# Hawk and HGRN2 trunk step: gate products as row tiles, Silu gates, two projections added in DRAM, the first layer's order searched as a whole

## The chip, the cores and the metric

The kernel runs on one core of one Trainium2 chip. The metric is the device time of one execution in microseconds (us). Engines: PE is the matrix engine (PEld its weight loads), DVE the vector engine, ACT the activation engine, POOL the general engine, SP the queue that issues most transfers.

## What is computed

One inference step of two layers over 1024 tokens of a new sequence and 8 sequences of 4 tokens each, 1056 columns in all, in float32. The first layer ("layer 1" in the title; `l0` in the code) is a recurrent one of width 1536 with gates that are block-diagonal, 16 blocks of 96; the second (`l1`) is a gated linear recurrence with matrix states. The change lies in the first.

```python
u = xn @ w_in                                   # 1024 -> 2 * 1536
xb, gate = u[..., :W_LRU], u[..., W_LRU:]
xc, new_buf = _causal_conv(xb, conv_w, conv_b, buf)
# _rg_lru, with xh = xc as 16 blocks of 96
r  = sigmoid(einsum('btni,nij->btnj', xh, w_r) + b_r)
ig = sigmoid(einsum('btni,nij->btnj', xh, w_i) + b_i)
log_a = -LRU_C * softplus(-lam) * r
a = exp(log_a)
bterm = sqrt(-expm1(2.0 * log_a)) * (ig * xc)
h = scan of h_t = a_t * h_(t-1) + bterm_t
y = h * silu(gate)
x = x + y @ w_out                               # 1536 -> 1024
```

## The kernel before

Everything is held with channels on the 128 partitions and tokens along the rows: `x` is 8 tiles of 128 x 1056, cut into three chunks `c` of 352 columns (`CH`). Each float32 operand is split into a high and a low part, and a product is three matmuls, high by high, high by low, low by high (`mm3`, lines 269 to 271). A block of 1024 x 128 weights is loaded in two transfers, its high part is made by a copy on ACT (L418) and its low part by a subtraction on POOL or DVE (L358).

The 1536 channels of the first layer are worked through in four groups `g` of 384, that is three tiles `j` of 128. For each group: `conv(g)` and `gate(g)` project the normalized input (24 matmuls to an output tile and chunk, psum banks `mm`, four of them); `lru(g)` does the gates and the recurrence; `split_y(g)` splits the result; `out(g)` multiplies by the group's rows of `w_out`, for groups 0 and 1, and `out_last` does groups 2 and 3 together.

The gates in `lru`. A group is four blocks of 96. Tile `j` holds block `j` in 96 of its rows and a third of the fourth block in the other 32 (rows 32j to 32j+31). For each chunk and each of the two gates (`i`), three products of 128 x 128 weights (`gh`, `gl`, with zeros where rows of the fourth block stand) use the three tiles of `X`; a fourth of 96 x 96 (`gsh`, `gsl`) uses the rows of the fourth block, which transfers have first gathered in `G4` (L344, six per chunk). Each product has its own bank of the four `hg`, and ACT takes it out with a Tanh (L618, L624). Then ACT does Exp, Tanh and a Sqrt (L631, L633, L641), DVE and POOL the products around them, and DVE the scan (L658).

The output gate (`gate`, L574 and 575) is ACT's Tanh of half the value and DVE's (t + 1) times the value; the missing factor 0.5 comes in where the state is multiplied on (L668). Where the input's norm is not known yet (`by`) or the state is there already (`late`), there are two DVE instructions.

`out(g, src, dst)` (L682 ff.): for each of 8 output tiles and 3 chunks, a product of 9 matmuls into an `mm` bank, a load of the running sum's chunk from DRAM, DVE's add from psum (L689), and a store. Group 0 reads the input and writes `x1a`, group 1 reads `x1a` and writes `x1b`, `out_last` reads `x1b`.

The order of everything is not that of the code. Each step is recorded in a `Flow` with its engine, an estimated duration, what it reads and writes and a priority. `plan` plays the steps through with these durations, one queue for each engine, and so makes an order; `run` repeats that eight times with keys from a pass backwards, then `search` shifts keys in the first 60 us at random, 3000 times, and keeps what gets more of PE's work done by then. The instructions are written out in that order on each engine. `plan` takes Tanh, Exp and Silu for one table of ACT and Sqrt for another, with 1.29 us for a swap (`SETS`, `SWAP`); a product of the gates is 0.48 us of PE.

Of the kernel before, what the change touches and what calls it, by code (L numbers as in the profile page):

```python
# [25 lines left out]
SEARCH = 3000  # L26
NW, NXO, NRAW = 4, 3, 3
# [27 lines left out]
class Flow:  # L55
# [56 lines left out]
    def plan(self, key, horizon=None):  # L112
# [13 lines left out]
        for _ in range(n):  # L126
# [84 lines left out]
    def run(self, tries=0, first=0.0):  # L211
        self.after = [[] for _ in self.ops]
        for i, o in enumerate(self.ops):
            for d in o[3]:
                self.after[d].append(i)
        best = got = self.plan([o[4] for o in self.ops])
        for _ in range(self.TURNS):
            got = self.plan(self.back(got[2], got[4]))
            self.ends.append(got[0])
            best = min(best, got, key=lambda g: g[0])  # L220
        if tries:
            best = self.search(best, tries, first)
        self.log = [(i, self.ops[i][0], best[1][i], best[2][i]) for i in best[3]]
        for i in best[3]:
            self.ops[i][2]()
# [12 lines left out]
def tile_trunk(ctx: ExitStack, tc: tile.TileContext, xT, prm, hc, w0, wg, wo0, w1, wo1, s_in,  # L238
# [91 lines left out]
    with ExitStack() as l0:  # L330
# [59 lines left out]
        G4 = fixed("G4", [96, NCH, CH], F32R)  # L390
# [164 lines left out]
        def gate(g, js=range(3), late=False):  # L555

            items = []
            for j in js:

                def evac(c, ps, pk, by=None, j=j):  # L560
                    sg, sk = sgs[g][j, c] = halves[g % 2][3 * j + c]
                    if late:
                        t, tk = next(ts)
                        act(CH, lambda: S.activation(t, ps[:, :CH], AF.Tanh, scale=0.5), (pk,), (tk,), 0)
                        dve(CH, lambda: V.scalar_tensor_tensor(t, t, 1.0, ps[:, :CH], op0=ALU.add, op1=ALU.mult), (pk, tk), (tk,), 0)
                        dve(CH, lambda: V.scalar_tensor_tensor(sg, sg, 0.5, t, op0=ALU.mult, op1=ALU.mult), (tk, sk), (sk,), 1, True)
                        return
                    if by:
                        t, tk = next(ts)
                        dve(CH, lambda: V.tensor_tensor(sg, ps[:, :CH], by[0], op=ALU.mult), (pk, by[1]), (sk,), 0)  # L570
                        act(CH, lambda: S.activation(t, sg, AF.Tanh, scale=0.5), (sk,), (tk,), 0)
                        dve(CH, lambda: V.scalar_tensor_tensor(sg, t, 1.0, sg, op0=ALU.add, op1=ALU.mult), (tk, sk), (sk,), 1, True)
                        return
                    act(CH, lambda: S.activation(sg, ps[:, :CH], AF.Tanh, scale=0.5), (pk,), (sk,), 0)  # L574
                    dve(CH, lambda: V.scalar_tensor_tensor(sg, sg, 1.0, ps[:, :CH], op0=ALU.add, op1=ALU.mult), (pk, sk), (sk,), 0)

                items.append((w0[ML + 3 * g + j], evac))
            return items

        def lru(g):  # L580
# [16 lines left out]
            for c in range(NCH):  # L597
# [6 lines left out]
                for j in range(3):  # L604
# [5 lines left out]
                for i, hb in ((0, hbr), (1, hbi)):  # L610
                    for j in range(3):
                        m = 3 * g + j
                        ps, pk = next(hg)
                        (a, ak), (b, bk) = xpart(j, 0, c), xpart(j, 1, c)
                        u = 3 * i + j
                        fl.add("PE", 0.48, lambda ps=ps, a=a, b=b, u=u: mm3(ps[:, :CH], (gh[:, u, :], gl[:, u, :]), a, b, True, True),
                               (ak, bk, ("gh", u // 4 * 4), ("gl", u // 4 * 4)), (pk,), 0)
                        act(CH, lambda ps=ps, R=R, i=i, j=j, hb=hb, m=m: S.activation(R[:, i, j], ps[:, :CH], AF.Tanh, bias=hb[:, m:m + 1],  # L618
                                                                           scale=0.5), (pk, ("smb",)), (("R", s, i, j),), 2, 0.1)
                    ps, pk = next(hg)  # L620

                    fl.add("PE", 0.48, lambda ps=ps, i=i, both=both: mm3(ps[:96, :CH], (gsh[:, i], gsl[:, i]), *both, True, True),
                           (("gsh",), ("gsl",), *(("g4", j, q) for j in range(3) for q in own)), (pk,), 0)
# [21 lines left out]
                for j in range(3):  # L645
# [22 lines left out]
                    dve(CH, lambda h=h, sg=sg: V.scalar_tensor_tensor(sg, h, 0.5, sg, op0=ALU.mult, op1=ALU.mult), (hk, sk), (sk,), 3, True)  # L668
# [11 lines left out]
        def out(g, src, dst):  # L680

            own = cycle([next(xos) for _ in range(NXO)] + [next(ts) for _ in range(3)] + [(x[:, :CH], k) for x, k in (next(xbs) for _ in range(3))])  # L682
            for m in range(KD):
                w = weights(wo0[m][:, 384 * g:384 * g + 384], 384)
                for c in range(NCH):
                    ps, pk = product(w, ycols(c))
                    x, xk = next(own)
                    dma(x, src[m][:, chunk(c)], ((g, m, c),), (xk,), 3)
                    dve(CH, lambda x=x, ps=ps: V.tensor_tensor(x, ps[:, :CH], x, op=ALU.add), (pk, xk), (xk,), 0)  # L689
                    dma(dst[m][:, chunk(c)], x, (xk,), ((g + 1, m, c),), 3)  # L690
                    yield

# [10 lines left out]
        def out_last(src):  # L703
# [42 lines left out]
            for c in range(NCH):  # L746
                acc = next(xbs)
                rows = []
                for i, m in enumerate(ms[c]):
                    ps, pk = product(blocks[m].get, ycols(c) + xcols(c)[:3], 1)  # L750
                    x, xk = spare[c][m]
                    dma(x, src[m][:, chunk(c)], ((2, m, c),), (xk,), 3)
# [220 lines left out]
        x1b = [nc.dram_tensor(f"x1b_{m}", (128, TOK), F32, kind="Internal").ap() for m in range(KD)]  # L973
# [4 lines left out]
        gates, rest = project0(gate(2)), out(0, xT, x1a)  # L978
# [8 lines left out]
        rest = out(1, x1a, x1b)  # L987
# [8 lines left out]
        out_last(x1b)  # L996
# [4 lines left out]
        with tc.manual_schedule(engines={E.PE, E.DVE, E.Activation, E.Pool, E.SP}):  # L1001
            fl.run(SEARCH, 60.0)


    with ExitStack() as l1:
# [865 lines left out]
        with tc.manual_schedule(engines={E.PE, E.DVE, E.Activation, E.Pool, E.SP}):  # L1871
            fl.run(SEARCH, 60.0)
# [71 lines left out]
```

## Time and profile before

| | |
|---|---|
| three timed runs | 1031.18, 1028.95, 1027.11 us (median 1028.95) |
| profiled execution, first to last instruction | 1027.8 us |
| PE busy in it | 1015.8 us (99%) |
| DVE, ACT, POOL busy | 808.0, 573.2, 504.2 us |
| first layer | to about 518 us |

No separate time is given for the profiled execution; its span is 1.15 us below the median of the timed ones. How to read the rows that follow: a row of a timeline is start, duration, engine, line, operation, what is written from what is read, the weights' rows * columns, the operand's shape and how many such rows were merged into one. In a table of groups, what stands between the bars is busy us and the mean ns of one, and behind the second bar the idle time of the engine just before and what ended it. Waits are: us in total, times, longest. Matmuls overlap, so the pace of PE is the distance between starts and not a duration. A matmul whose operands are plain float32 shows as two records.

### The profile page before, as it was taken

How to read it: one execution, taken by the hardware profiler on the slowest of the kernel's cores; microseconds unless marked ns; L12 is line 12 of the kernel's file. 1: busy time of each engine (PE TensorE's matmuls, PEld its weight loads, DVE VectorE, ACT ScalarE, POOL GpSimd, SP SyncE). 2: the span in 40 equal slices, each digit the busy share in tenths (PEclk: the TensorE clock that was granted, in tenths of full speed). 3: DMA queues.
4: the chain of work that ended last, by engine and by line, in shares of the span. 5: the costliest groups of instructions: out<-in, count | busy, mean ns of one | idle time of the engine just before them, and what ended most of it. 6: DMA issues, size and time to landing. Idle time of an engine off the chain costs nothing.

```text
span 1027.8 us, 26439 instructions
## 1 busy us (share of the span) xinstructions
PE 1015.8 (99%) x10100; PEld 995.2 (97%) x10100; DVE 808.0 (79%) x1640; ACT 573.2 (56%) x1313; POOL 504.2 (49%) x580
## 2 busy tenths in 40 slices
PE   9999999999999999999999999999999999999997
PEld 9999999999999999999999999999999999999986
DVE  7998987689788689344598989888989898986436
ACT  7688566877765766344454463626363545552324
POOL 1324454454446345635425555555565656633544
PEclk9999999999999999999999999999999999999999
DMA  9211112213762487553564245443535353777204
GB/s 303 73 51 37 54 57 66 79 53 104 222 198 70 131 267 241 157 173 130 159 192 136 72 131 149 130 148 112 167 107 172 94 166 114 217 230 229 88 1 169
DMA packets 109582, 139.95 MB, mean 136 GB/s; under 512 B 24208, under 2 KB 86800, under 8 KB 109456
## 3 DMA queue, kind: packets, MB, share of 16 engines
q1 hardware_dynamic: 107440, 135.84, 42.7%
q10 hardware_dynamic: 2016, 2.43, 0.7%
q8 instruction: 79, 1.29, 0.5%
q14 instruction: 47, 0.39, 0.1%
HBM read 90.02 MB, written 41.61 MB: 128 GB/s over the span
## 4 chain that ended last, share of the span: by engine, by line
PE 87%; DVE 4%; DMA 4%; ACT 2%; issue 1%; POOL 1%; SPq 1%; POOLq 0%; ACTq 0%; DVEq 0%
PE mm L269 25%; PE mm L271 24%; PE mm L270 24%; PE hg L1138 2%; DMA R<-td 1%; PE hg L269 1%; PE hg L270 1%; PE hg L271 1%; PE hg L1340 1%; PE hg L1285 1%; PE hg L1342 1%; DMA wraw<-in_w_dram 1%; DMA k<-x1a 1%; SPq L344 1%; DMA R<-in_xT_dram 1%
## 5 line engine op out<-in xcount | busy, mean ns | idle before, releaser
L269 PE MATMUL mm<-xh,whi 128*128 128x352 f32 (+1 forms) x1127 | 349.9, 311 | 0.0
L271 PE MATMUL mm<-xh,wlo 128*128 128x352 f32 (+1 forms) x1127 | 347.8, 309 | 0.0
L270 PE MATMUL mm<-xl,whi 128*128 128x352 f32 (+1 forms) x1127 | 347.7, 309 | 0.0
L358 POOL TENSOR_TENSOR wlo<-wraw,whi 128x256 fp32r<-128x256 f32 (+3 forms) x188 | 201.9, 1090 | 194.6 <-ACT whi L418 93.7
L269 PEld LDWEIGHTS mm<-xh,whi 128*128 128x128 f32 x1127 | 211.7, 188 | 1.2 <-DVE k L1598 0.2
L270 PEld LDWEIGHTS mm<-xl,whi 128*128 128x128 f32 x1127 | 212.3, 188 | 0.4
L271 PEld LDWEIGHTS mm<-xh,wlo 128*128 128x128 f32 x1127 | 212.0, 188 | 0.0
L269 PE MATMUL mm<-t,whi 128*128 128x264 f32 (+1 forms) x330 | 96.6, 293 | 0.0
L544 DVE SCALAR_TENSOR_TENSOR k<-xb,prm_sb,k 128x352 f32<-128x352 f32 (+2 forms) x144 | 87.3, 633 | 10.4 <-ACT k L541 9.6
L271 PE MATMUL mm<-t,wlo 128*128 128x264 f32 (+1 forms) x330 | 94.5, 286 | 0.0
L270 PE MATMUL mm<-t,whi 128*128 128x264 f32 (+1 forms) x330 | 94.3, 286 | 0.0
L1598 DVE TENSOR_TENSOR k<-mm,k 128x264 f32<-128x264 f32 x154 | 64.1, 424 | 11.9 <-PE mm L271 10.5
L358 POOL TENSOR_TENSOR wlo<-R,whi 128x256 fp32r<-128x256 f32 x70 | 57.1, 838 | 27.8 <-ACT whi L1522 24.6
L1522 ACT CAST whi<-wraw 128x512 fp32r<-128x512 f32 x56 | 34.6, 617 | 58.6 <-DVE wraw L1532 31.0
L637 POOL TENSOR_TENSOR k<-X 128x352 f32<-128x352 f32 x36 | 43.8, 1222 | 45.4 <-DVE R L638 33.6
L269 PEld LDWEIGHTS mm<-t,whi 128*128 128x128 f32 x330 | 62.0, 188 | 2.1 <-ACT kt L1355 0.9
L271 PEld LDWEIGHTS mm<-t,wlo 128*128 128x128 f32 x330 | 62.2, 188 | 0.0
L270 PEld LDWEIGHTS mm<-t,whi 128*128 128x128 f32 x330 | 62.1, 188 | 0.0
L418 ACT CAST whi<-wraw 128x512 fp32r<-128x512 f32 (+2 forms) x79 | 43.8, 571 | 27.3 <-PE mm L270 20.0
L269 PE MATMUL mm<-yh,whi 128*128 128x352 f32 x153 | 49.9, 326 | 1.0 <-DVE k L689 1.0
L270 PE MATMUL mm<-yl,whi 128*128 128x352 f32 x153 | 49.4, 323 | 0.0
L271 PE MATMUL mm<-yh,wlo 128*128 128x352 f32 x153 | 49.4, 323 | 0.0
(484 smaller groups left out, 2503.1 us busy)
## 6 DMA issues: line engine op xcount, KB each, us to landing
wraw<-in_w_dram SPq DMA_DIRECT2D x89, 256.0 KB, 3.1
wraw<-in_wo_dram SPq DMA_DIRECT2D x34, 192.0 KB, 2.6
R<-in_w_dram SPq DMA_DIRECT2D x17, 256.0 KB, 3.5
si<-in_s_in_dram SPq DMA_DIRECT2D x8, 512.0 KB, 5.5
vt<-sg SPq DMA_DIRECT2D x8, 512.0 KB, 3.7
kt<-kt SPq DMA_DIRECT2D x8, 512.0 KB, 3.3
sg<-vt SPq DMA_DIRECT2D x32, 128.0 KB, 2.9
kt<-kt SPq DMA_DIRECT2D x32, 128.0 KB, 4.5
```

Of the source, the lines that this page charges most:

```text
L269: T.matmul(out, wh, xh, start=first, stop=False)
L270: T.matmul(out, wh, xl, start=False, stop=False)
L271: T.matmul(out, wl, xh, start=False, stop=last)
L344: fl.add("SP" if q is Q else "ACT", us, lambda: q.dma_start(dst, src), r, w, prio, kb * (1.0 if r else 0.75))
L358: emit = lambda: e.tensor_tensor(b, x, a.bitcast(F32), op=ALU.subtract)
L418: act(m, lambda hi=hi, raw=raw, m=m: S.copy(hi[:, :m], raw[:, :m]), rk, (hk,), prio)
L544: dve(u, lambda src=src, dst=dst, sh=sh, k=k: V.scalar_tensor_tensor(dst, sh(src, k), pc("cw", 12 * k + m), dst, op0=ALU.mult, op1=ALU.add ...
L637: pool(CH, lambda x=x, a=a, b=b: G.tensor_tensor(x, a.bitcast(F32), b.bitcast(F32), op=ALU.add), (ak, bk), (xk,), 3)
L1138: T.matmul(ps[32 * j:32 * j + 32, n * w:n * w + w], B[:, o:o + 32], q(slice(o, o + 32)), start=True, stop=True, tile_position=(0, 32 * j))
L1285: T.matmul(ps[w, n * 128:(n + 1) * 128], kt[:, 4 * i + n, a], vt[:, 4 * i + n], start=True, stop=True, tile_position=(0, 32 * a))
L1522: act(512, lambda: S.copy(hi, raw), (rk,), (hk,), 2)
L1598: dve(QT, lambda: V.tensor_tensor(o[0], z[0], u[0], op=ALU.add), (z[1], u[1]), (o[1],), 0)
```

## The change

Five things, all in the first layer:

- **Gates.** The rows of the array are cut into tiles, so that matmuls on few rows can share a pass. The block-diagonal weights have no zeros multiplied any more: the four products of a chunk and gate become three slots. A slot is one step of PE for the planner (0.48 us) and has three passes (high by high, high by low, low by high). In slots 1 and 2 a pass is two matmuls of 64 rows, in slot 3 four of 32 rows, each with its own bank; the four products are ready when slot 3 is done, and they need all four `hg` banks at once. `G4` needs only two of the three row pieces (four transfers for six); the third is read where it is.
- **Silu.** ACT computes the output gate in one instruction; the factor 0.5 and DVE's part go.
- **Projections.** `out(g)` no longer loads and adds: ACT copies the product out of psum, a transfer stores it in `part[g][m]`, and when three chunks are there, a transfer that adds in DRAM, issued by POOL, adds the tile to `x1a[m]`. `x1a` starts as a copy of the input, by eight transfers from DRAM to DRAM. `x1b` is gone.
- **Search.** `refine` shifts keys of steps of the whole first layer, 3000 times, and keeps an order whose planned end is not later. The second layer has none.
- In the planner, POOL's transfers are no longer held up by DVE's use of the shared memory port.

```diff
+REFINE = 3000, 0
...
-            elif e == "POOL":
+            elif e == "POOL" and not kb:
...
+    def refine(self, best, tries):
+
+        rng, key, end = Random(2), list(best[1]), best[0]
+        free = [i for i, o in enumerate(self.ops) if o[4] >= 0]
+        for _ in range(tries):
+            t, w = rng.uniform(0.0, best[0]), rng.choice((5.0, 10.0, 20.0))
+            near = [i for i in free if abs(key[i] - t) < w]
+            if not near:
+                continue
+            new = list(key)
+            for i in rng.sample(near, min(len(near), rng.randint(1, 6))):
+                new[i] += rng.gauss(0.0, rng.choice((2.0, 6.0, 15.0)))
+            got = self.plan(new)
+            if got[0] <= end + 1e-9:
+                end, key = got[0], list(got[1]) if rng.random() < 0.5 else new
+                best = min(best, got, key=lambda g: g[0])
+        return best
...
-                    act(CH, lambda: S.activation(sg, ps[:, :CH], AF.Tanh, scale=0.5), (pk,), (sk,), 0)
-                    dve(CH, lambda: V.scalar_tensor_tensor(sg, sg, 1.0, ps[:, :CH], op0=ALU.add, op1=ALU.mult), (pk, sk), (sk,), 0)
+                    act(CH, lambda: S.activation(sg, ps[:, :CH], AF.Silu), (pk,), (sk,), 0)
...
-                for j in range(3):
+                for j in range(2):
...
                 for i, hb in ((0, hbr), (1, hbi)):
+                    got = [next(hg) for _ in range(4)]
+                    xs = [[xpart(j, p, c) for p in range(2)] for j in range(3)]
+                    four = [(both[p], [("g4", j, own[p]) for j in range(2)]) for p in range(2)]
+
+                    def slot(*tiles, i=i, got=got, first=False, last=False):
+
+                        cells, r = [], []
+                        for b, x, rows in tiles:
+                            q = slice(*rows)
+                            w = (gsh[q, i], gsl[q, i]) if b == 3 else (gh[q, 3 * i + b, :], gl[q, 3 * i + b, :])
+                            cells.append((got[b][0][:96 if b == 3 else 128, :CH], *w, x[0][0][q], x[1][0][q], rows[0]))
...
+                        def emit():
+                            for k, (u, v) in enumerate(((1, 3), (1, 4), (2, 3))):
+                                for t in cells:
+                                    T.matmul(t[0], t[u], t[v], start=first and not k, stop=last and k == 2, tile_position=(t[5], 0))
+
+                        fl.add("PE", 0.48, emit, r, [got[b][1] for b, _, _ in tiles], 0)
+
+                    slot((2, xs[2], (0, 64)), (0, xs[0], (64, 128)), first=True)
+                    slot((1, xs[1], (64, 128)), (3, four, (0, 64)), first=True)
+                    slot((1, xs[1], (0, 32)), (0, xs[0], (32, 64)), (3, xs[2], (64, 96)), (2, xs[2], (96, 128)), last=True)
...
-                    dma(x, src[m][:, chunk(c)], ((g, m, c),), (xk,), 3)
-                    dve(CH, lambda x=x, ps=ps: V.tensor_tensor(x, ps[:, :CH], x, op=ALU.add), (pk, xk), (xk,), 0)
-                    dma(dst[m][:, chunk(c)], x, (xk,), ((g + 1, m, c),), 3)
+                    act(CH, lambda x=x, ps=ps: S.copy(x, ps[:, :CH]), (pk,), (xk,), 0)
+                    dma(part[g][m][:, chunk(c)], x, (xk,), (("part", g, m, c),), 3)
                     yield
+                fl.add("POOL", 1.0, lambda m=m: G.dma_start(x1a[m], part[g][m], accum_op=ALU.add, max_dma_last_dim=8192),
+                       [("part", g, m, c) for c in range(NCH)], [("x1a", m)], 5, 540)
...
+        for m in range(KD):
+            dma(x1a[m], xT[m], (("xh", m, 2),), (("x1a", m),), 6, 700)
```

PE before, at the gates of the first group: products of the gates (`hg`, from `X`) stand between those of a convolution tile (`mm_159`).

```order
L271 MATMUL mm_159<-xh_97,X_142 128x352
L269 MATMUL hg_163<-X_142,gh_117 128x352 [waits Activation_49]
L270 MATMUL hg_163<-X_142,gh_117 128x352
L271 MATMUL hg_163<-X_142,gl_118 128x352
L269 MATMUL hg_164<-X_142,gh_117 128x352 [waits Activation_49]
L270 MATMUL hg_164<-X_142,gh_117 128x352
L271 MATMUL hg_164<-X_142,gl_118 128x352 [waits Pool_49]
```

All of them use the whole array. PE in the change, the last slot of 64 rows in a run and the start of the slot of 32 rows (L646 is the matmul of a slot; `hg_161` to `hg_164` are the four banks, `gh` and `gl` the weights' parts):

```order
L646 MATMUL hg_161<-X_142,gl_118 128x352
L646 MATMUL hg_163<-X_142,gl_118 128x352
L646 MATMUL hg_164<-X_142,gh_117 128x352
L646 MATMUL hg_163<-X_142,gh_117 128x352
L646 MATMUL hg_162<-X_142,gsh_119 96x352
L646 MATMUL hg_161<-X_142,gh_117 128x352
L646 MATMUL hg_164<-X_142,gh_117 128x352
```

Two matmuls to a pass have become four. A run of L646 is mostly a whole set of 24 (15 times); the 576 of them stand in 34 runs, between matmuls on all rows.

ACT before, in the gates of the first group (L574 is the Tanh of the output gate, L631 Exp, L633 Tanh, L618 and L624 take the gates out of psum):

```order
L574 ACTIVATE sg_147<-mm_159 128x352
L631 ACTIVATE a_114<-R_73,smalls_84 128x352 [waits DMAHW1_49]
L618 ACTIVATE R_73<-hg_164,smalls_84 128x352 [waits PE_49]
L618 ACTIVATE R_73<-hg_161,smalls_84 128x352 [waits PE_49]
L624 ACTIVATE td_116<-hg_162,smalls_84 96x352 [waits PE_49]
L633 ACTIVATE R_73<-R_73,smalls_84 128x352 [waits Activation_49]
L574 ACTIVATE sg_145<-mm_160 128x352
```

No table load stands between them. ACT in the change, at a like place later in the layer (L592 is Silu, L656 and L659 take the gates out of psum, L666 is Exp, L668 Tanh, L676 Sqrt):

```order
L666 ACT_TABLE_LOAD [waits DMAHW5_49]
L666 ACTIVATE a_114<-R_73,smalls_84 128x352 [waits Activation_49]
L666 ACTIVATE a_114<-R_73,smalls_84 128x352 [waits DMAHW6_49,Activation_49]
L656 ACTIVATE R_73<-hg_161,smalls_84 128x352 [waits DMAHW4_49,PE_49]
L666 ACTIVATE a_114<-R_73,smalls_84 128x352 [waits DMAHW0_49,Activation_49]
L659 ACTIVATE td_116<-hg_162,smalls_84 96x352
L668 ACTIVATE R_73<-R_73,smalls_84 128x352 [waits Activation_49]
L656 ACTIVATE R_73<-hg_164,smalls_84 128x352
L668 ACTIVATE R_73<-R_73,smalls_84 128x352
L656 ACTIVATE R_73<-hg_163,smalls_84 128x352
L592 ACT_TABLE_LOAD
L592 ACTIVATE sg_146<-mm_159 128x352 [waits PE_49]
```

A table load now stands at each step between Exp and Silu; the program has 48 table loads, against 30.

More of the change, by code (lines that the diff above doesn't have):

```diff
@@ L209, in search, with run @@
         return min(best, self.plan(key), key=lambda g: g[0])
-    def run(self, tries=0, first=0.0):
+    def refine(self, best, tries):
[14 more added lines that the diff above has]
+        return best
+    def run(self, tries=0, first=0.0, more=0):
         self.after = [[] for _ in self.ops]
@@ L222, in run @@
             best = self.search(best, tries, first)
+        if more:
+            best = self.refine(best, more)
         self.log = [(i, self.ops[i][0], best[1][i], best[2][i]) for i in best[3]]
@@ L610, in lru @@
                 for i, hb in ((0, hbr), (1, hbi)):
+                    got = [next(hg) for _ in range(4)]
[7 more added lines that the diff above has]
+                            cells.append((got[b][0][:96 if b == 3 else 128, :CH], *w, x[0][0][q], x[1][0][q], rows[0]))
+                            for p in range(2):
+                                r += x[p][1] if isinstance(x[p][1], list) else [x[p][1]]
+                            r += [("gsh",), ("gsl",)] if b == 3 else [(n, (3 * i + b) // 4 * 4) for n in ("gh", "gl")]
+                        def emit():
[3 more added lines that the diff above has]
+                        fl.add("PE", 0.48, emit, r, [got[b][1] for b, _, _ in tiles], 0)
@@ L622, in lru @@
-                    fl.add("PE", 0.48, lambda ps=ps, i=i, both=both: mm3(ps[:96, :CH], (gsh[:, i], gsl[:, i]), *both, True, True),
-                           (("gsh",), ("gsl",), *(("g4", j, q) for j in range(3) for q in own)), (pk,), 0)
+                    ps, pk = got[3]
                     act(CH, lambda ps=ps, i=i: S.activation(td[:, i], ps[:96, :CH], AF.Tanh, bias=hbd[:96, 4 * i + g:4 * i + g + 1],
@@ L972, in tile_trunk @@
         yd = [nc.dram_tensor(f"yd_{h}", (128, TOK), F32, kind="Internal").ap() for h in range(H - 2)]
-        x1b = [nc.dram_tensor(f"x1b_{m}", (128, TOK), F32, kind="Internal").ap() for m in range(KD)]
+        part = [[nc.dram_tensor(f"part_{g}_{m}", (128, TOK), F32, kind="Internal").ap() for m in range(KD)] for g in range(2)]
+        for m in range(KD):
+            dma(x1a[m], xT[m], (("xh", m, 2),), (("x1a", m),), 6, 700)
         lru(0)
@@ L977, in tile_trunk @@
         run(project0(conv(1)))
-        gates, rest = project0(gate(2)), out(0, xT, x1a)
+        gates, rest = project0(gate(2)), out(0)
         run(islice(gates, 6))
@@ L986, in tile_trunk @@
         run(project0(gate(3,(0,))))
-        rest = out(1, x1a, x1b)
+        rest = out(1)
         run(project0(conv(3)))
@@ L1001, in tile_trunk @@
         with tc.manual_schedule(engines={E.PE, E.DVE, E.Activation, E.Pool, E.SP}):
-            fl.run(SEARCH, 60.0)
+            fl.run(SEARCH, 60.0, REFINE[0])
     with ExitStack() as l1:
@@ L1871, in tile_trunk @@
         with tc.manual_schedule(engines={E.PE, E.DVE, E.Activation, E.Pool, E.SP}):
-            fl.run(SEARCH, 60.0)
+            fl.run(SEARCH, 60.0, REFINE[1])
 def _cols(a):
```

26 lines of the change are left out of this document (9 added, 17 removed).

## The prediction

> **What bounds the kernel now.** I read the page first, then the table of stretches, then the list of who waited for whom on PE.
>
> ```profile
> span 1027.8 us, 26439 instructions
> PE 1015.8 (99%) x10100; PEld 995.2 (97%) x10100; DVE 808.0 (79%) x1640; ACT 573.2 (56%) x1313; POOL 504.2 (49%) x580
> ```
>
> ```profile
> core 0: us, PE busy (x) PEld busy (x) DVE busy (x) ACT busy (x) POOL busy (x), PEclk, DMA share, GB/s
> 0.00:518.00 518.00, 514.47 (x3179) 510.53 (x3180) 388.59 (x735) 332.57 (x671) 231.79 (x262) 1.00 0.43 133
> 518.00:1027.80 509.80, 501.30 (x6923) 484.63 (x6921) 419.36 (x906) 240.62 (x642) 272.44 (x318) 1.00 0.46 140
> ```
>
> ```profile
> PE hg L783 <- DVE nr L378: 1.0, 1, 1.0
> PE mm L269 <- DVE k L689: 1.0, 3, 0.5
> ...
> PE hg L270 <- DMA G<-X: 0.6, 1, 0.6
> ...
> PE hg L269 <- ACT R L618: 0.5, 1, 0.5
> ```
>
> The first recurrent layer, which the title calls layer 1, ends at about 518 us. In it PE is busy for 514.5 of 518 us at clock 1.00, while ACT and DVE have 185 and 129 us to spare. PE waits for others hardly at all: the three waits that belong to the gates and to the projections that the change touches (DVE L689, DMA into G, ACT L618) are 2.1 us together. So what the change does to the time is, first, what it does to the length of PE's own queue.
>
> A busy PE hides its real pace, since a matmul of 0.32 us overlaps the next ones. The pace is the distance of starts. The first and the last of 79 further starts, all of 352 columns (timeline of PE):
>
> ```profile
> 7.72 0.32 PE L270 MATMUL mm<-xl,whi 128*128 128x352 f32 x1
> ...
> 20.44 0.33 PE L271 MATMUL mm<-xh,X 128*128 128x352 f32 x1
> ```
>
> (20.44 - 7.72) / 79 = 0.161 us for one matmul of 352 columns.
>
> **Gates in three passes.** Today a product of the gates is three matmuls over all 128 rows (or 96) of the array:
>
> ```profile
> L269 PE MATMUL hg<-X,gh 128*128 128x352 f32 x72 | 23.4, 325 | 0.5 <-ACT R L618 0.5
> ...
> L269 PE MATMUL hg<-G,gsh 96*96 96x352 f32 x24 | 7.8, 324 | 0.0
> ```
>
> 72 + 24 products of three are 288 matmuls, in 24 sets (four groups of channels, three chunks, two gates) of 12. Afterwards a set is three slots of three passes; a pass holds two matmuls of 64 rows or four of 32 rows that should run side by side. If they do, a set costs 9 starts instead of 12: 72 x 0.161 = 11.6 us less.
>
> Do tiles run side by side? The trace has tiles of columns (the 32 behind the star), not of rows:
>
> ```profile
> 581.25 0.28 PE L271 MATMUL mm<-xh,wlo 128*128 128x264 f32 x1
> 581.45 1.08 PE L1285 MATMUL mm<-sg,kt 128*32 128x128 f32 x32
> 582.35 1.06 PE L1285 MATMUL hg<-sg,kt 128*32 128x128 f32 x32
> ```
>
> 32 records of 128 columns take 582.35 - 581.45 = 0.90 us, 0.11 for each four. A single record over all columns costs as much (L1380 below, 0.87 / 8 = 0.11). So four tiles go for one. I take the same for tiles of rows.
>
> The price is in going from one way of cutting the array to another. Two places where the trace does that, the second from two views:
>
> ```profile
> 546.41 0.32 PE L271 MATMUL mm<-xh,wlo 128*128 128x352 f32 x1
> 546.67 0.46 PE L1216 MATMUL hg<-R,a 128*32 128x32 f32 x32
> 547.05 0.69 PE L1223 MATMUL hg<-R,sg 128*64 128x64 f32 x16
> 547.67 0.43 PE L269 MATMUL mm<-xh,whi 128*128 128x352 f32 x1
> 547.94 0.32 PE L270 MATMUL mm<-xl,whi 128*128 128x352 f32 x1
> ```
>
> ```profile
> 971.59 0.87 PE hg L1380 x8
> ```
>
> ```profile
> 971.43 1.03 PE L1380 MATMUL hg<-ident,kt 128*128 128x128 f32 x8
> ```
>
> ```profile
> 972.40 0.24 PE L1385 MATMUL hg<-ident,ons 32*128 32x32 f32 x1
> 972.57 0.43 PE L269 MATMUL mm<-xh,whi 128*128 128x352 f32 x1
> 972.84 0.32 PE L270 MATMUL mm<-xl,whi 128*128 128x352 f32 x1
> ```
>
> All are rows of PE's timeline but the L1380 x8 of 0.87 us, which is the chain's. Into column tiles, L1216 starts 0.26 us after a matmul that is worth 0.16: 0.10 lost. Into a tile of 32 rows, L1385 should start at 971.43 + 0.87 = 972.30 and starts at 972.40: 0.10 lost, and this is the only kind of row tile in the trace. Behind each change back, the first full matmul holds the second for 0.27 instead of 0.16: 0.11 lost, which I read as its 128 columns of weights loading in the open, since nothing runs before them. The new tiles have 96 or 128 columns too, so I charge 0.10 + 0.11 = 0.21 us for each change of cut.
>
> How many are there? In the new order of PE the 576 short matmuls stand in 34 runs: 68 changes at their two ends, and 21 inside, where a slot of 32 rows follows one of 64 (15 whole sets, 6 runs of two slots that hold the step). 89 x 0.21 = 18.7 us. The bounds are 89 x 0.10 = 8.9, if the loads hide, and 89 x 0.25 = 22.3, if two or four loads get in each other's way a little. So the gates come out at -11.6 + 18.7 = +7.1 us.
>
> TensorE: Matmul & The Clock Gate, in the Trainium skill, speaks against the change more softly (Part 3, Measured speedup vs the span model): four row tiles reached 3.07 times, not 4 times, the speed of one after the other. By that, an estimate, each of the 72 passes with four tiles costs 1.30 matmuls, 72 x 0.30 x 0.161 = 3.5 us more, and the sum below would be 1039, inside the main case; no run so far shows four row tiles.
>
> **Silu.** One ACT instruction replaces ACT's Tanh and removes one DVE instruction for each of 36 gate tiles. ACT gets the copies of the two projections in exchange, 2 x 8 x 3 = 48, and DVE loses its 48 adds.
>
> ```profile
> L641 ACT ACT_TABLE_LOAD x12 | 15.4, 1283 | 0.2
> L528 ACT COPY xb<-mm 128x352 f32<-128x352 f32 (+1 forms) x33 | 14.5, 440 | 23.9 <-PE mm L271 23.8
> ```
>
> ```profile
> L575 DVE SCALAR_TENSOR_TENSOR sg<-sg,mm 128x352 f32<-128x352 f32 x27 | 13.7, 512 | 14.5 <-ACT sg L574 14.5
> ...
> L689 DVE TENSOR_TENSOR k<-mm,k 128x352 f32<-128x352 f32 x18 | 9.2, 518 | 6.0 <-DMA k<-in_xT_dram 3.2 <-PE mm L271 1.8 <-DMA k<-x1a 0.8
> ```
>
> DVE loses 36 x 0.51 + 48 x 0.52 = 43 us; ACT gains 48 x 0.44 = 21 us. ACT gains something that the planner does not know: it counts Silu and Exp as one table, but the new order has a table load at nearly every step between them, 48 loads against 30. That is 18 x 1.283 = 23 us. ACT goes to 333 + 21 + 23 = 377 of 518 us, so it does not become the bound; each load can delay what is queued behind it by 1.28 us. In front of PE this matters where a set waits for the four banks of the set before it: nine of the 23 distances between sets in PE's order are 36 matmuls (5.8 us) or less, in which ACT has four evacuations to do. The bounds are 0 and 18 x 1.28 = 23 us; I take 1, near the low end, because PE itself is 18.7 / 24 = 0.8 us per set later than the planner thinks.
>
> **Projections added in DRAM.** The loads of the old sum go away, and with them the waits of L689: 1.0 us, and the wait for the shortened copies into G and for ACT behind them, up to 2.1 us in all. I take 1.5. The 16 accumulating transfers stand on POOL's queue, each behind three stores; behind them wait the low halves of weights (L358). Rows for transfers of that size:
>
> ```profile
> yd<-sg SPq DMA_DIRECT2D x6, 528.0 KB, 3.8
> ...
> x1a<-ST SPq DMA_DIRECT2D x9, 176.0 KB, 3.3
> ```
>
> A store lands in 3.3 us, 528 KB in 3.8; an addition that reads both sides I bound by 3.8 and three times that, 11.4. Out of the way of PE both: the last projection that reads the sum begins after the late gates (six blocks of 24 matmuls, 23 us). Nothing for PE unless POOL stands still behind a store; the cover is POOL's idle half (232 of 518 us busy). The eight copies of the input at the start stand on SP ahead of weights: 8 x 3.8 = 30 us of landings at worst if they didn't overlap, hidden by two blocks of weights ahead (2 x 11.6 us); overlapping, nothing.
>
> **Search over the whole order.** It can remove only waits that exist: 3.5 us of idle PE in the layer, of which 1.0 is the start. Beyond the 1.5 above I count nothing.
>
> **Sum.** -11.6 + 18.7 + 1.0 - 1.5 = +6.6 us. The profiled execution spans 1027.8 us; the three timed runs have the median 1028.95, 1.15 us around it, which stays. 1028.95 + 6.6 = 1035.5 us. With the bounds of the terms it is 1024 (8.9, ACT 0, 2.1 recovered) to 1042 (22.3, ACT 4).
>
> **Rivals.**
> 1. Changes of cut are free, or nearly, for rows: then faster. For it: 96-row matmuls come and go without a gap.
>
> ```profile
> 360.18 0.32 PE L271 MATMUL mm<-yh,wlo 128*128 128x352 f32 x1
> 360.34 0.32 PE L269 MATMUL hg<-G,gsh 96*96 96x352 f32 x1
> 360.50 0.32 PE L270 MATMUL hg<-G,gsh 96*96 96x352 f32 x1
> ```
>
> Against it: 96 rows need no other cut than 128 do, and L1385 with 32 rows lost its 0.10. At 0.03 a change: -11.6 + 2.7 - 2.1 = -11, 1018 us. It decides at 11.6 / 89 = 0.13 us a change; below that the gates gain.
> 2. ACT's table loads hold PE: half of the 18 in full, 11.5 us, on top of the main case without its 1.0: 1046. Against it: ACT is idle a third of the layer.
> 3. The loads of weights for two or four row tiles go one after the other. A load in the open cost 0.11 above, so a pass of two would take 0.22, of four 0.44, instead of 0.161: 24 x (6 x 0.06 + 3 x 0.28) = 29 us more, 1064. Against it: four loads fit into the 0.11 us of L1285, but those have 32 columns each.
> 4. The row tiles do not run side by side: the change does not do what it says. 576 - 216 = 360 starts more, 58 us: 1093.
>
> **Chances.** Main case 0.48; rival 1 0.24; rival 2 0.12; rival 3 0.12; rival 4 0.04. The range 1017 to 1048 holds the main case, nearly all of rival 1 and most of rival 2, about 0.80. A half per cent, 5.1 us, is about what a measurement of this kernel can tell from no change: faster means below 1023.8, slower above 1034.1. Rival 1 gives 0.21 of faster and the low end of the main case 0.01; of the main case 0.22 lie within, with 0.03 of rival 1 and 0.01 of rival 2; the rest, 0.52, is slower. The likeliest case's own range is 1024 to 1042.
>
> **What would show it.** In PE's timeline: starts of 0.161 us between the passes of a slot (rival 3: 0.22 and 0.44; rival 4: every matmul 0.161 apart); at the edges of a run of row tiles 0.10 lost and then 0.11 (rival 1: none); the first layer's end near 524 instead of 518 us. On ACT: about 48 table loads and 377 us busy. In PE's waits: no L689, no DMA into G; a sum of waits on ACT over 5 us would mean rival 2. The gates' term is wrong if a whole set, with what is lost at its edges, takes less than the 12 x 0.161 = 1.93 us of today; the sum is wrong without it if waits of PE, not its own work, make the difference.

## The result: 1056.3 us, 2.6% slower

| | before | after |
|---|---|---|
| median of 4 runs, us | 1029.59 (1027.11 to 1031.18) | 1056.28 (1054.24 to 1057.90) |
| ratio to before, 95% interval | 1 | 1.0256 (1.0235 to 1.0277) |
| profiled execution: span, us | 1027.8 | 1056.1 |
| end of the first layer (first matmul of L1138, now L1176), us | 518.3 | 543.9 |
| second layer, us | 509.5 | 512.2 |
| matmuls | 10100 | 10388 |
| ACT's table loads | 30 | 48 |

The change is slower by 26.7 us, where 6.6 were predicted, and lies outside the range. Of the 28.3 us of the spans, 25.6 are in the first layer. The page's first line of busy times, and the stretch of the first layer (granted clock, DMA share and GB/s last):

```profile
PE 1031.3 (98%) x10388; PEld 988.2 (94%) x10388; DVE 774.8 (73%) x1556; ACT 611.4 (58%) x1379; POOL 515.6 (49%) x596
```

```profile
0.00:543.90 543.90, 528.52 (x3469) 502.84 (x3469) 357.07 (x652) 371.04 (x737) 242.68 (x278) 0.99 0.46 132
```

PE is not busy for 15.4 us of the first layer, where it was for 3.5, and the clock is no longer 1.00. ACT came out near what was worked out, 371 us for 377; DVE is busy for 357, 32 less than before where 43 less were worked out. The list of who waited for whom on PE (total, times, longest) names what PE stood for:

```profile
PE hg L646 <- DMA G<-X: 4.4, 1, 4.4
PE mm L292 <- POOL wlo L750: 2.1, 1, 2.1
PE mm L290 <- ACT xb L552: 2.1, 1, 2.1
PE mm L290 <- ACT k L585: 1.9, 1, 1.9
PE hg L519 <- DVE k L517: 1.5, 3, 0.7
```

The waits that the prediction wanted to recover (L689, 1.0 us) are gone, and larger ones stand at other places: a gate set that waits for its gathered rows (`G<-X`), and projections that wait for ACT and for low halves from POOL. The longest, in the chain of what waited for what (start, duration, step):

```profile
379.79 6.91 DMA part<-k
...
386.71 5.89 DMA G<-X
...
392.74 0.58 PE hg L646
```

The gather itself took 5.9 us, and by this chain it was started only when a store of a product, 6.9 us long, had landed.

**The gates themselves.** PE's timeline around one whole set of 24 row tiles (a row's first number is its start):

```profile
102.65 0.32 PE L292 MATMUL mm<-xh,wlo 128*128 128x352 f32 x1
102.90 0.42 PE L646 MATMUL hg<-X,gh 64*128 64x352 f32 x1
...
103.16 0.32 PE L646 MATMUL hg<-X,gh 64*128 64x352 f32 x1
...
104.06 0.42 PE L646 MATMUL hg<-X,gh 32*128 32x352 f32 x2
104.06 0.40 PE L646 MATMUL hg<-X,gsh 32*96 32x352 f32 x1
104.07 0.42 PE L646 MATMUL hg<-X,gh 32*128 32x352 f32 x1
...
104.32 0.33 PE L646 MATMUL hg<-X,gh 32*128 32x352 f32 x3
...
104.48 0.33 PE L646 MATMUL hg<-X,gl 32*128 32x352 f32 x3
104.74 0.43 PE L290 MATMUL mm<-xh,whi 128*128 128x352 f32 x1
105.01 0.32 PE L291 MATMUL mm<-xl,whi 128*128 128x352 f32 x1
```

Four row tiles start within 0.01 us of each other and the next four 0.16 later (104.32, 104.48): they do run side by side. Going in costs 0.25 (102.65 to 102.90) and 0.26 (to 103.16) where 0.16 each would be due, going out 0.26 and 0.27. From the last full matmul to the second full one after the set are 105.01 - 102.65 = 2.36 us; less two of 0.161 for these, the set costs 2.04 us, against 12 x 0.161 = 1.93 before. That is nine passes and three changes of cut of 0.2 us.

**The clock.** After the wait for `G<-X`, stretches of 3.41 us each (PE busy and matmuls first, then PEld, DVE, ACT, POOL, the granted clock, DMA share, GB/s):

```profile
388.97:392.38 3.41, 0.00 (x0) 0.00 (x0) 0.00 (x0) 3.38 (x8) 1.59 (x2) 1.00 1.04 242
392.38:395.79 3.41, 3.05 (x19) 2.26 (x20) 1.03 (x2) 1.38 (x4) 0.93 (x1) 0.50 1.00 260
395.79:399.21 3.42, 3.42 (x13) 3.42 (x13) 0.55 (x2) 1.90 (x5) 1.33 (x2) 0.50 0.48 162
399.21:402.62 3.41, 3.41 (x22) 3.41 (x22) 1.45 (x1) 3.13 (x6) 3.36 (x4) 1.00 0.55 127
```

PE stands for one stretch, and the clock is then 0.50 for two. The first of them holds the set's short matmuls too; in the second, all of full matmuls, 13 fit where 22 do afterwards. Each such stretch costs about 9 x 0.155 = 1.4 us. The first layer has four (351.42, 392.38, 395.79, 440.17), the second one (948.75); before had none between its start and 1023 us.

So the 25.6 us are about 6 of changes of cut, 12 of waits (the five rows above and four of 0.6 to 0.7 make 14.5; the old 2.1 are gone) and 5 to 6 of half clock; 1 to 3 stay unassigned. What makes the waits was the question for the experiments.

### The profile page after: what moved, and what is told of

The parts are those of the page before. It is cut to its first block, busy times and chain, and to the rows that moved or that the text cites. A ratio compares the mean times of both kernels' runs of the same rounds, so it can differ in the third digit from the quotient of the medians.

```text
span 1056.1 us, 26937 instructions
## 1 busy us (share of the span) xinstructions
PE 1031.3 (98%) x10388; PEld 988.2 (94%) x10388; DVE 774.8 (73%) x1556; ACT 611.4 (58%) x1379; POOL 515.6 (49%) x596
## 4 chain that ended last, share of the span: by engine, by line
PE 71%; DVE 11%; ACT 7%; DMA 6%; issue 2%; POOL 2%; SPq 0%; POOLq 0%; ACTq 0%; DVEq 0%
PE mm L290 20%; PE mm L292 19%; PE mm L291 19%; PE hg L646 3%; DVE k L565 2%; DMA R<-td 2%; PE hg L1176 2%; DMA part<-k 1%; DMA G<-X 1%; DVE R L693 1%; PE hg L1323 1%; PE hg L1378 1%; DMA k<-yd 1%; PE hg L1380 1%; ACT a L666 1%
## 5 line engine op out<-in xcount | busy, mean ns | idle before, releaser
L379 POOL TENSOR_TENSOR wlo<-wraw,whi 128x256 fp32r<-128x256 f32 (+3 forms) x188 | 198.8, 1075 | 196.3 <-ACT whi L1560 85.4
L565 DVE SCALAR_TENSOR_TENSOR k<-xb,prm_sb,k 128x352 f32<-128x352 f32 (+2 forms) x144 | 91.1, 656 | 14.6 <-ACT k L562 13.8
L1636 DVE TENSOR_TENSOR k<-mm,k 128x264 f32<-128x264 f32 x154 | 64.1, 424 | 12.6 <-PE mm L292 11.3
L673 DVE SCALAR_TENSOR_TENSOR R<-R,k 128x352 f32<-128x352 f32 x36 | 25.9, 736 | 45.0 <-DMA R<-td 42.2
L290 PE MATMUL mm<-yh,whi 128*128 128x352 f32 x153 | 52.7, 344 | 0.0
```

The lines of the kernel that those rows point to most:

```text
L290: T.matmul(out, wh, xh, start=first, stop=False)
L379: emit = lambda: e.tensor_tensor(b, x, a.bitcast(F32), op=ALU.subtract)
L565: dve(u, lambda src=src, dst=dst, sh=sh, k=k: V.scalar_tensor_tensor(dst, sh(src, k), pc("cw", 12 * k + m), dst, op0=ALU.mult, op1=ALU.add ...
L673: dve(CH, lambda x=x, j=j, ti=ti: V.scalar_tensor_tensor(ti[:, j], ti[:, j], 1.0, x, op0=ALU.add, op1=ALU.mult), (xk, tik[j]), (tik[j],), ...
L1636: dve(QT, lambda: V.tensor_tensor(o[0], z[0], u[0], op=ALU.add), (z[1], u[1]), (o[1],), 0)
```

## The experiments

Three theories beside the changes of cut. **Tables**: ACT's 18 more table loads make it late for PE. **Additions**: the 16 adding transfers of 528 KB crowd the transfer engines, and what PE waits for lands late. **Search**: an order searched to the planner's last tenth is too tight for real durations. Ratios are to the kernel before, run on the same chip; the last column is (ratio - 1) x 1030 us.

| run | what stays of the change | ratio (95%) | us over before |
|---|---|---|---|
| the change | all | 1.0256 (1.0235 to 1.0277) | +26.4 |
| a1_tanh_for_silu | all, same order, no more table loads | 1.0147 (1.0121 to 1.0173) | +15.1 |
| a2_small_adds | all, same order, additions of 16 columns | 1.0144 (1.0116 to 1.0172) | +14.8 |
| a4_tanh_small_adds | both | 1.0069 (1.0050 to 1.0089) | +7.1 |
| a5_plain_copies | all, same order, copies for additions | 1.0132 (1.0115 to 1.0149) | +13.6 |
| a3_full_rows | all, same order, no change of cut | 1.0249 (1.0223 to 1.0275) | +25.6 |
| b1_no_search | all but the search | 1.0248 (1.0227 to 1.0268) | +25.5 |
| b3_old_gates | all but row tiles | 1.0202 (1.0177 to 1.0226) | +20.8 |
| b5_old_tanh_gates | all but Silu | 1.0135 (1.0113 to 1.0157) | +13.9 |
| b2_search_alone | search | 1.0000 (0.9989 to 1.0012) | 0.0 |
| c1_row_tiles_alone | row tiles, search | 1.0057 (1.0042 to 1.0072) | +5.9 |
| b6_dram_adds_alone | additions, search | 1.0059 (1.0036 to 1.0082) | +6.1 |
| c2_silu_alone | Silu, search | 1.0133 (1.0118 to 1.0149) | +13.7 |
| c2h_silu_planner_told | Silu, search; two tables planned | 1.0057 (1.0037 to 1.0077) | +5.9 |
| b6h_adds_told | additions, search; dearer in the plan | 1.0113 (1.0090 to 1.0137) | +11.6 |
| h1_tables_told | all; two tables planned | 1.0244 (1.0202 to 1.0285) | +25.1 |
| h2_planner_told | all; three prices planned | 1.0303 (1.0279 to 1.0327) | +31.2 |

### In the changed kernel's own order

**a1_tanh_for_silu.**

```diff
-S.activation(sg, ps[:, :CH], AF.Silu)
+S.activation(sg, ps[:, :CH], AF.Tanh)
...
```

> The changed kernel in its own order, with ACT's Tanh written where Silu stood (the output gates are then wrong: Silu is left out). Tanh is in the table of Exp, so 18 of the 48 table loads, 23 us of ACT, go and nothing else moves. If the table loads make ACT late and PE waits for that: at least half of the 19 us that neither the changes of cut nor the old waits explain goes, 1046 us or less. If the adding transfers crowd the queues, or the order is too tight for the real times: within 3 us of the changed kernel's 1056, and PE's long wait for the copy into G (4.4 us at 388 us) stays.

1044.4 us, 11 less than the change: the theory of the tables holds for that much. Its waits of PE:

```profile
PE hg L646 <- DMA G<-X: 3.3, 1, 3.3
PE mm L292 <- POOL wlo L750: 2.4, 1, 2.4
```

The waits for ACT (L552, L585) are gone, with the half clock behind them; the wait for `G<-X` stays, as the theory of the additions says.

**a2_small_adds.**

```diff
-G.dma_start(x1a[m], part[g][m], accum_op=ALU.add, max_dma_last_dim=8192)
+G.dma_start(x1a[m][:, :16], part[g][m][:, :16], accum_op=ALU.add, max_dma_last_dim=8192)
```

> The changed kernel in its own order, but each of the 16 transfers that add to x1a moves 16 columns of 1056 (most of the addition of the first two projections is left out). The same number of transfers stand at the same places. If their bytes crowd the transfers that PE waits for: the wait of 4.4 us for the copy into G goes, with the half clock behind it, and the time falls by 7 to 14 us, to 1042 to 1049. If ACT's table loads or a tight order make the waits: within 3 us of 1056.

1045.9 us, 11.5 less: the mirror image. The wait for `G<-X` is gone, and the waits for ACT stay:

```profile
PE mm L292 <- POOL wlo L750: 2.3, 1, 2.3
PE mm L290 <- ACT xb L552: 2.0, 1, 2.0
...
PE mm L290 <- ACT k L585: 1.3, 1, 1.3
```

Why it is the transfers is seen in the view of the queues, in the stretch from 360 to 420 us of the changed kernel and of a2 (packets, MB and share of 16 engines; then issues with KB and median us to landing):

```profile
q0 software_dynamic: 896, 4.33, 43.5%
q1 hardware_dynamic: 6873, 8.72, 41.7%
...
x1a<-part POOLq DMA_DIRECT2D x8, 528.0 KB, 7.3
...
R<-td SPq DMA_DIRECT2D x13, 44.0 KB, 5.5
...
G<-X SPq DMA_DIRECT2D x6, 44.0 KB, 5.4
```

```profile
R<-td SPq DMA_DIRECT2D x15, 44.0 KB, 1.9
...
G<-X SPq DMA_DIRECT2D x5, 44.0 KB, 2.1
```

Eight of the sixteen additions fall into these 60 us and take 43.5% of all transfer engines. The small transfers beside them, the rows gathered for the gates (`G<-X`) and those given back behind them (`R<-td`), take two to three times as long to land.

**a4_tanh_small_adds.** Both edits.

> The edits of a1_tanh_for_silu and a2_small_adds together (Silu and most of the addition left out), in the changed kernel's order. If table loads and bytes of the adding transfers together make the late waits and the half clock behind them: 1036 to 1040 us, that is the kernel before plus the 6 us of the changes of cut plus 2. If the searched order is too tight for the real durations whatever they are: over 1046, with waits at other places.

1037.5 us. The 7.1 us that are left are the changes of cut and about one more; no stretch before 1027 us is at half clock. ACT's 48 copies and the stores to `part` are still there, so they cost hardly anything by themselves. PE's wait for POOL's low half (L750, 2.3 us) is still there too: neither cause makes it, and what does was not tried. The two causes together took 19.3 us; one by one 11.3 and 11.6, so about 3.6 us come only where both are there.

**a5_plain_copies.**

```diff
-G.dma_start(x1a[m], part[g][m], accum_op=ALU.add, max_dma_last_dim=8192)
+G.dma_start(x1a[m], part[g][m], max_dma_last_dim=8192)
```

> The changed kernel in its own order, with each of the 16 adding transfers turned into a plain copy of the same 528 KB to the same place by the same queue (the sums of the first two projections with the input are left out). If it is the adding, that is more time of the transfer engines for a byte than a copy takes, that crowds what PE waits for: the queue's share of the 16 engines falls from 5.0% of the span to under 3.5%, the copies land sooner than the additions' 7.3 us, and 5 to 10 us go, 1046 to 1051. If it is the bytes at this place alone: no less than 1053.

1043.9 us: 12.8 us go, more than the theory asked for, and as much as in a2. The same bytes at the same places, as plain copies, cost PE no more than a2's 16 columns do. The queue's row in the page:

```profile
q0 software_dynamic: 1792, 8.65, 2.8%
```

The additions have 5.0% of a span of 1056.1 us in 16 transfers, that is 0.050 x 1056.1 / 16 = 3.3 us of all sixteen engines for each; a copy has 0.028 x 1046.4 / 16 = 1.8 us. They land after 7.3 and 4.9 us. So it is not the 528 KB as such, but what adding takes on top of copying them.

**a3_full_rows.**

```diff
-for k, (u, v) in enumerate(((1, 3), (1, 4), (2, 3))):
-    for t in cells:
-        T.matmul(t[0], t[u], t[v], start=first and not k, stop=last and k == 2, tile_position=(t[5], 0))
...
+for b, wl, xl_, st, sp in passes:
+    T.matmul(got[b][0][:96 if b == 3 else 128, :CH], w(b, wl), x(b, xl_), start=st, stop=sp)
```

> The changed kernel in its own order, with nine matmuls on all rows for the 24 row tiles of a set (part of the gate products is left out, other parts counted twice), so that no change of cut is left. By the trace a set then takes 9 x 0.161 = 1.45 us instead of 2.05, 24 x 0.6 = 14 us less on PE. If the rest of the order has room: 1042 us. If the waits for ACT, POOL and transfers set PE's end there, a part of the 14 us comes back as longer waits, since PE then comes earlier to each of them: 1048 us or more.

What the edit leaves out is three of a set's twelve partial products and a third of the fourth block's rows; nothing is counted twice; the expectation is wrong there. 1055.1 us: of the 14 us of PE's work that it removes, 0.8 is gained (within the intervals, nothing). The waits say where the rest went:

```profile
PE hg L651 <- DMA G<-X: 14.3, 6, 4.5
PE hg L651 <- ACT R L661: 3.1, 2, 2.8
```

With additions and table loads in place, PE is no longer the bound of this part: it comes earlier to the same landings, and waits.

### Planned anew, one part at a time

**b1_no_search** and **b2_search_alone** (`REFINE` 0, 0 in the changed kernel; `refine` and its call in the kernel before).

> The changed kernel without the search over the whole order (REFINE is 0 for both layers), planned anew; the row tiles, Silu and the additions in DRAM stay, and it has 54 table loads instead of 48. If the search made an order that is too tight for the real durations: 1046 us or less. If table loads, adding transfers and changes of cut make the loss by themselves: within 4 us of the changed kernel's 1056, and above rather than below.

> The kernel before, with the search over the whole order as the only change. If searched orders are too tight: 1034 us or more, with new waits of PE. If the search is harmless, since the kernel before has only about 3 us of waits to take away: 1027 to 1030, against 1030 of the kernel before.

1055.1 and 1029.5 us: the search neither harms nor helps. The theory of the tight order falls.

**b3_old_gates** and **b5_old_tanh_gates** (the four products of before in `lru`; the Tanh of before in `gate` with its DVE instructions).

> The changed kernel with the gate products of before (four products of three matmuls on all rows), planned anew; Silu (51 table loads) and the additions in DRAM and the search stay. If the three causes add up: the changed kernel's 1056 less the 6 us of the changes of cut, about 1050. If PE's delay by the changes of cut, which the planner does not know, is what turns the other two into waits: 1040 or less.

> The changed kernel with the output gates of before (ACT's Tanh, then DVE), planned anew; row tiles, additions in DRAM and the search stay, and there are 30 table loads as before. If the table loads cost what the run with Tanh for Silu in the fixed order gave: 1044 us. If the adding transfers then hit other places, since the order is another: 1038 to 1050, with a wait for a transfer or none as the only difference. If Silu costs nothing by itself and the order alone decided: 1053 or more.

1050.5 and 1043.1 us: without row tiles 5.6 less than the change, without Silu 12.5 less, in orders planned anew. That is close to what the changed kernel's own order gave (about 6 worked out from the trace, 11.3 by a1), so what these two are worth in the whole is no accident of one order.

**c1_row_tiles_alone, b6_dram_adds_alone, c2_silu_alone** (each keeps one part and takes the other two from the kernel before).

> The kernel before with the gates as row tiles and the search, without Silu and without the additions in DRAM, planned anew. If the causes add up and the changes of cut are worth what the trace of the changed kernel shows (a set takes 2.045 us instead of 1.932, with stalls apart 6 us): 1034 to 1038. If PE's unplanned delay by itself brings waits for ACT or transfers: 1040 or more. If the other parts had made the row tiles dearer: 1030 to 1033.

> The kernel before with the first two projections added in DRAM and the search, without row tiles and without Silu, planned anew. If the causes add up: about 10 us above the kernel before, 1038 to 1042. If the adding transfers hurt only because row tiles and table loads have left no room: 1030 to 1034.

> The kernel before with Silu for the output gates and the search, without row tiles and without the additions in DRAM, planned anew, so that table loads stand between Exp and Silu that the planner does not count. If the causes add up: about 12 us above the kernel before, 1040 to 1044. If table loads hurt only where the other parts have left no room: 1030 to 1034.

1035.6, 1035.5 and 1043.4 us, +5.9, +6.1 and +13.7: 25.7 together, against 26.4 of the whole. Row tiles alone end the first layer at 523.8 us, with the clock at 1.00 and no new wait above 0.7 us. The additions alone cost less than the 11.6 that they are worth in the whole, between the two times that were expected; that with PE and ACT less late they meet fewer waits is my reading. Their two longest waits of PE there are for ACT (2.1 and 1.3 us), but a late transfer stands behind the one that ends at 370.76 us:

```profile
361.31 7.18 DMA R<-td
```

ACT's next Exp starts at 368.52, when these 44 KB have landed, and ACT empties the bank that PE needs only behind it. Silu is the other way round, 13.7 alone and 11.3 to 12.5 in the whole, so it is partly luck that the sum fits better than its parts. Silu alone shows best what a table load does. PE and ACT at one place of c2_silu_alone:

```profile
203.57 0.32 PE L292 MATMUL mm<-xh,wlo 128*128 128x352 f32 x1
205.79 0.40 PE L290 MATMUL hg<-G,gsh 96*96 96x352 f32 x1 [1.90 <-ACT td L641]
```

```profile
203.54 1.28 ACT L592 ACT_TABLE_LOAD   x1
204.84 0.46 ACT L592 ACTIVATE sg<-mm 128x352 f32<-128x352 f32 x1
205.20 0.54 ACT L641 ACTIVATE td<-hg,smalls 96x352 f32<-96x352 f32 x1
```

PE needs a bank of the last set, which L641 empties; L641 stands behind Silu, and Silu behind its load. PE stands 1.90 us. In its first layer it is idle for 13.2 us, where it was for 3.5 before, and its largest waits are of this kind:

```profile
PE hg L290 <- ACT td L641: 4.9, 5, 1.9
PE hg L290 <- ACT R L635: 2.7, 4, 1.1
```

### The planner told

**c2h_silu_planner_told** and **h1_tables_told** (Silu alone; the whole change).

```diff
-SETS = {"Sqrt": 1, "Tanh": 2, "Exp": 2, "Silu": 2}
+SETS = {"Sqrt": 1, "Tanh": 6, "Exp": 2, "Silu": 4}
...
```

(The numbers become bits: Tanh is in both tables. The two places that compare them test bits.)

> Silu alone (gates of before, sums of before), with the planner told that Exp and Silu are two tables; it has 55 table loads where Silu alone had 50. If PE's waits for ACT there came from loads that the plan left out: 1032 to 1036, in spite of more loads. If the loads cost by their number: 1043 or more.

> The whole change, with the planner told only that Exp and Silu are two tables (57 loads instead of 48). If the plan's ignorance of the loads makes the same share of their cost here as for Silu alone, where 7.6 of 13.7 us went: 1047 to 1050. If the additions in DRAM leave no room for a plan to move ACT's work (as the run with all three prices told suggests): 1054 or more.

Silu alone falls from +13.7 to +5.9 us, though it has 55 loads instead of 50. So the number of loads isn't the price: a load that the plan sees is put where PE doesn't wait behind it. The longest wait for ACT in c2h is 0.8 us:

```profile
PE hg L292 <- ACT R L637: 3.3, 5, 0.8
```

In the whole change the same knowledge is worth nothing that can be told (1053.4 us; four runs from 1052.9 to 1061.4, the profiled one the longest): the theory that it would recover the same share there fell.

**b6h_adds_told** and **h2_planner_told**.

```diff
-[("part", g, m, c) for c in range(NCH)], [("x1a", m)], 5, 540)
+[("part", g, m, c) for c in range(NCH)], [("x1a", m)], 5, 1250)
...
-fl.add("PE", 0.48, emit, ...)
+fl.add("PE", 0.88 if last else 0.58, emit, ...)
```

(The first pair alone in b6h; both, and the tables, in h2.)

> The additions in DRAM alone (gates of before, output gates of before, the search), with the planner told 1250 KB for each instead of 540. If their 5.8 us come from a plan that books them too cheap: 1029 to 1032. If they cost by what they do to the transfers around them, wherever they stand: 1034 to 1037.

> The whole change, with the planner told what the traces show: Exp and Silu as two tables (46 loads in the program instead of 48), a slot of 64 rows as 0.58 us and one of 32 rows as 0.88 us of PE instead of 0.48 each, an addition in DRAM as 1250 KB of transfer instead of 540. If the loss is mostly waits that the planner could not see: 1040 or less, that is the 6 us of the changes of cut and a few more. If table loads and additions have no place where they are free: 1046 or more.

1042.0 and 1061.0 us: both are worse for being told, b6h above either time that was expected. In h2 PE waits 4.5 us for a late output gate (L587), and a stretch of 17 us from 433.6 us is at half clock. h1 has that wait too, 5.9 us in one piece, so it comes without the dearer additions. In b6h one of the two longest waits (3.0 us) is for a copy by ACT that, by the chain, stood behind a store to `part` of 8.1 us. The planner keeps transfers as one line of bytes, one after the other; that a dearer addition there delays what in the chip shares the engines is my reading, and which move in the order did it was not tried. No run beats the kernel before; the best with anything of the change but the search is 1035.5 us.

## Why the prediction was wrong, step by step

- **Gates: right.** Predicted -11.6 + 18.7 = +7.1 us at 0.21 for a change of cut; the trace shows 0.20, and row tiles alone measure +5.9 (4.3 to 7.4). The order of that run has 97 changes instead of 89, so that they come to (11.6 + 5.9) / 97 = 0.18 each. Rivals 1, 3 and 4 fall by the rows of the set above: changes aren't free, loads don't follow one another, and the tiles run side by side. Of the Trainium skill, TensorE: Matmul & The Clock Gate, Measured speedup vs the span model, gave 3.07 for four row tiles; here a pass of four takes 0.16 us like a pass of one, so the extra 3.5 us of that estimate did not come.
- **Silu, "the bounds are 0 and 18 x 1.28 = 23 us; I take 1": the step that failed.** Alone it measured +13.7 us, in the whole 11.3 to 12.5. The bounds held it. The reason for the low end was the mistake: PE's own 0.8 us per set was counted as cover. In c2 the waits stand where the working looked, at sets that wait for the banks of the set before: an evacuation behind a load of 1.3 us, an ACTIVATE of 0.46 and its own 0.5 holds PE for 1.90 us, more than 0.8 us could have covered. (c2 has no row tiles, so PE isn't late there; that the cover falls short is worked out, not measured.) In the whole change PE's two long waits for ACT stand elsewhere, at projections (L552, L585; 4.0 us), and no load stands directly ahead. From the chain behind the first, which ends at 165.43 us:

```profile
139.04 1.28 ACT L592
...
163.95 0.51 DVE k L565
...
165.43 0.43 PE mm L290
```

  By this chain a load makes ACT late for DVE, DVE works through a queue for 20 us, and ACT's copy waits behind an instruction that waits for DVE. a1, without the 18 loads, has neither wait. Rival 2 (half of 18 loads, 11.5 us) had the mechanism and the price, and got 0.12, "ACT is idle a third of the layer": an average, where the question was what stands in front of one instruction and behind it in other queues.
- **Additions, "nothing for PE unless POOL stands still": the second step that failed.** Alone +6.1, in the whole 11 to 13 us. The landing was inside its bounds (7.3 of 3.8 to 11.4). What was missed is that an addition takes from the transfers beside it: 3.3 us of all sixteen engines, in a stretch of which the profile before had a row that the prediction didn't ask for, 360 to 420 us:

```profile
q1 hardware_dynamic: 11244, 13.96, 73.5%
...
G<-X SPq DMA_DIRECT2D x3, 44.0 KB, 5.0
```

  At 73.5% and with `G<-X` already at 5.0 us there, instead of its median of 1.9, there was little room for eight additions. The cover that was named was POOL's idle half; the one that was needed was the engines'.
- **The eight copies at the start: right as far as seen.** No new wait of over 1 us stands in front of PE before 160 us; they were not tried by themselves.
- **Search and old waits, -1.5: 0 measured** (search alone 1.0000). The waits for L689 went, others took their place.
- **Left out altogether: the clock.** About 6 of the 25.6 us are PE at half clock after its waits. The prediction priced a wait at its own length.
- **The sum.** With the measured terms in the prediction's own sum: 5.9 + 13.7 + 6.1 + 0 = 25.7 us; 1029.6 + 25.7 = 1055.3, against 1056.3. "The sum is wrong without it if waits of PE, not its own work, make the difference" is what happened, and the cost of rival 2 and that of the additions come on top of each other: the prediction weighed rivals as if only one could come. That the three measured terms meet the whole within 1 us is partly luck, since the additions alone cost about half of what they cost in the whole.

## What to carry to other kernels

Ask of an engine that is idle a third of the time not how busy it is but what stands in its queue directly ahead of the instruction that the bound engine waits for, as the table load in c2 does, and then what other queues that instruction waits for: in the whole change a load was paid 25 us later, by way of DVE. Price a transfer by what it takes from all transfer engines in its own stretch, and look up how full that stretch is and which small gathers share it. A planner that searches harder with a wrong price finds nothing: here the search was worth 0, and one right price was worth 7.8 us to one part alone and nothing to the whole.

## What the runs showed of the hardware

**Half clock after a wait of about 2 us.** Stretches at half clock are 3.41 us long or twice that (a 17 us one in h2) and begin on a grid of 3.41 us. One begins behind this stretch of the changed kernel, in which PE was busy for 1.46 of 3.41 us, and none behind the next, busy for 1.67:

```profile
436.76:440.17 3.41, 1.46 (x10) 1.17 (x9) 3.41 (x4) 1.60 (x4) 3.41 (x4) 1.00 0.39 116
440.17:443.58 3.41, 3.41 (x13) 3.41 (x13) 2.68 (x5) 2.10 (x6) 3.41 (x7) 0.50 0.41 130
```

```profile
163.69:167.10 3.41, 1.67 (x10) 1.67 (x11) 2.88 (x8) 2.62 (x9) 1.48 (x2) 1.00 0.31 92
167.10:170.52 3.42, 3.42 (x23) 3.42 (x22) 3.35 (x5) 3.11 (x8) 3.20 (x6) 1.00 0.08 18
```

Over the 18 profiled runs, all 28 grid stretches with 1.83 us or more of standing were followed by one at half clock; of the 40 with 1.0 to 1.8 us, 11 were. So whether a wait of 2 us costs 1.4 us more depends on where it falls on the grid. The Trainium skill, TensorE: Matmul & The Clock Gate, Part 1, has the free-running window of 3413 ns and names an idle window as what lowers the clock; the trace agrees with the length, and half an idle window was enough here.

**A table load costs what its record says.** From the changed kernel's ACT:

```profile
425.04 1.00 ACT L656 ACTIVATE R<-hg,smalls 128x352 f32<-128x352 f32 x2
426.06 1.28 ACT L585 ACT_TABLE_LOAD   x1
427.35 0.82 ACT L585 ACTIVATE k<-mm 128x352 f32<-128x352 f32 x2
```

From the end of one ACTIVATE (426.04) to the start of the next (427.35) are 1.31 us. ScalarE: Activation LUTs, What ACT_TABLE_LOAD costs, of the Trainium skill, counts a drain on top, 2.66 us in all; no such drain shows here. Silu's table holds Tanh and not Exp: Tanh runs behind either without a load. In the changed kernel a Tanh (L659) starts at 141.03 us behind a Silu of 140.34 without one, and in ACT's order in the change, shown ahead of the prediction, L656, L659 and L668 (Tanh) follow L666 (Exp) without one, while L592 (Silu) behind them has one.

**Adding is dearer than copying.** DRAM to DRAM, 528 KB: 3.3 us of all sixteen engines and 7.3 us to landing in the changed kernel, against 1.8 and 4.9 for the copy in a5.
